# First layer's PLE gate as seven block products, with operands made in the MLP's first pass

## The chip, the cores and the metric

The kernel runs on one core of one Trainium2 chip. The metric is device time in microseconds of one execution. The engines are named as in the profile: PE (TensorE, matmuls; PEld its weight loads), DVE (VectorE), ACT (ScalarE), POOL (GpSimd), SP (SyncE, which here only issues DMAs).

## The reference

Two layers on 1024 tokens with 1024 features. Each layer mixes tokens (layer 0: a gated MLP and a gated delta rule; layer 1: differential attention), then an MLP with squared ReLU, then the PLE step, which the change concerns in layer 0:

```
hn = rms_norm(h, ln_mlp[layer])
h = h + square(relu(hn @ w_mlp1[layer])) @ w_mlp2[layer]
gate = sigmoid(rms_norm(h, ln_ple[layer]) @ w_ple_gate[layer])   # 1024 x 1024
h = h + (p[layer] @ w_ple_proj[layer]) * gate                    # p: 1024 x 256
```

## The kernel before

Activations stand with features on partitions: `acc[m][h]` is feature block m (8 of 128) and token half h (2 of 512). Float32 accuracy comes from splitting every operand into a high part (an ACT cast) and a low part (a DVE subtraction), `split`, L265; `mm3`, L249, then makes three matmuls, high x high, high x low and low x high, each 128x128 by 128x512. The scale of rms_norm is a factor per token and is applied behind the product (`rb[h]`, a row of 512 factors copied to all partitions; `rms`, L300, with `far` sends it through DRAM by two DMAs).

The kernel is written with a tile framework. A tile takes one of its tag's buffers: the rings `w` (12 buffers of 128x512) and `raw` (8), and the slots `c0` to `c13`, `d0`, `B`, `A0` to `A5`, of one buffer each. A new tile under a tag waits until every reader of the old one is done. The framework makes the semaphores and orders each engine's instructions in advance by a timeline that it works out, earlier program text first where several are ready. Each engine then works in that fixed order.

**The MLP** (L333) is two passes of a seven-product block scheme (Strassen's, in Winograd's form). The first pass makes g in 8 chunks of 512 hidden features. A chunk's work is five products of 24 matmuls (`rest`, L472, chunks 0 to 4, named s3, s2, a22, s1, a12 by their left operands in the code) or seven (`chained`, L509, chunks 5 to 7, which also open the next chunk: s2, s1, s3, open1, a22, open2, a12). `product` (L391) splits the weights, then issues 24 matmuls into two PSUM banks. The last product of a chunk, a12, is accumulated into the banks whose earlier content `plus(g22, ...)` has read into the tile g22. `work` (L445) places g12, g21, g22 in the slots c8 to c13: g22 is in c12 and c13, and leaves them when `combine` (L456) has stored it. The seven operands of the second pass go to DRAM by SP's queue (`save`). Between chunks 1 to 4 a side job, `prepare` (L236), makes split attention weights by way of POOL's DMA queue. The second pass (`product2`, L606) runs seven products of 16 steps with 12 matmuls each and gives `acc`; ahead of it `split_p` (L675) transposes p.

**The PLE** (`ple`, L702) is a plain product: for both halves and each feature block m, 8 contraction tiles x 3 = 24 matmuls into a bank. The weights are loaded and split 256 columns at a time, once for each half. `close` (L706) follows: 6 matmuls of the p projection into an `aux` bank (two buffers), then on DVE, ACT, DVE, DVE: times rb, tanh, (1 + t) times the projection, and the sum into acc; a store of h by SP's queue, and `add_square` for the next norm. `put_h` (L277) makes the split operands of the next stage, `values` (L746), which multiplies them with part of the attention weights.

Of the kernel before, what the change touches and what calls it, by code (L numbers as in the profile page):

```python
# [11 lines left out]
F32 = mybir.dt.float32  # L12
# [6 lines left out]
P = 128  # L19
# [26 lines left out]
def f32(ap):  # L46
    return ap.bitcast(F32)
# [92 lines left out]
class Trunk:  # L140
# [107 lines left out]

    def mm3(self, ps, a, b, first, last, more=False):  # L249
# [83 lines left out]
    def mlp(self, x, x_tags, gain, w1, w2, gain_next, h_dram, p, last, side=iter(())):  # L333
# [42 lines left out]
        us, g11s, marks = {}, {}, []  # L376
# [172 lines left out]
        for c in range(NCH):  # L549
            (rest if c < 5 else chained)(c)  # L550
# [10 lines left out]

        pT = self.split_p(p)
# [102 lines left out]
        else:  # L665
            product2(2, y, True)
            add(0, 1, y, put)
            product2(4, x, False, rms)
            self.mlp_mark = self.pe.mark
            add(4, 1, x, put)  # L670
        self.hs[1] = self.hs_new[1]
# [30 lines left out]
    def ple(self, pT, acc, wg, wpj, gain_next, h_dram):  # L702
        nc = self.nc
        gates = []

        def close():  # L706
            h, m, ps = gates.pop(0)
# [4 lines left out]
            nc.vector.tensor_tensor(t, ps, rb[h], ALU.mult)  # L712
# [7 lines left out]
        hs, rb, sqs = list(self.hs), list(self.rb), self.sqs[1]  # L720
        self.new_hs()
        for h in range(2):
            for j in range(4):
                w = self.weight(wg[:, j * 256 : (j + 1) * 256], KT, 256)
                for ml in range(2):
                    m = 2 * j + ml
                    ps = self.mm_ps()
                    for k in range(KT):
                        self.mm3(ps, w.at(k, slice(ml * P, (ml + 1) * P)), hs[h][k], k == 0, k == KT - 1)
                    n = KT * h + m  # L730
                    if n == 0:
                        wq = [self.weight_p(wpj, i) for i in range(4)]
                    if n == 2:
                        rb[1] = self.rms(1, sqs, far=True)[1]
                    while len(gates) > (n < 3):
                        close()
                    gates.append((h, m, ps))
            close()
            for m in range(KT):
                self.put_h(m, h, acc[m][h], gain_next[:, m : m + 1])  # L740
            if h == 0:
                self.take_hs(0, rows=False)
        self.hs[1] = self.hs_new[1]
# [1522 lines left out]
def trunk(tc, x, p, ln_mix_e, w_in_e, gmlp_v_gain, gmlp_ws, gmlp_bs, gdn_conv, gdn_a_log, gdn_dt_bias, gdn_out_gain,  # L2266
          w_out_e, ln_mix_o, w_qkv_o, attn_q_gain, attn_k_gain, diff_lambda, attn_sub_gain, w_out_o, ln_mlp, w_mlp1,
          w_mlp2, ln_ple, w_ple_gate, w_ple_proj, masks, out):
    with ExitStack() as ctx:
# [60 lines left out]
        for layer in range(2):  # L2330
# [18 lines left out]
            acc, pT = T.mlp(x, ((ACC[0:2], ACC[2:4]) if layer else (("A1", "A0"), ("A2", "A3"))), gain[3 * layer + 1], w_mlp1[layer], w_mlp2[layer], gain[3 * layer + 2], h_dram, p[layer, 0], layer == 1, T.prepare(w_qkv_o[0]) if layer == 0 else iter(()))  # L2349
# [4 lines left out]
            T.ple(pT, acc, w_ple_gate[0], w_ple_proj[0], gain[3], h_dram)  # L2354
# [45 lines left out]
```

## Time and profile before

| | |
|---|---|
| median of 3 runs | 2490.58 us (2490.25 to 2491.13) |
| the profiled execution | 2489.38 us |
| its span, first to last instruction | 2487.3 us |
| PE, DVE, ACT, POOL busy | 2476.5, 1828.6, 1341.6, 284.2 us |
| HBM read, written | 318.23 MB, 133.18 MB |
| first pass of the first MLP | till about 775 us |
| its second pass | from 777 to about 1089 us |
| first PLE | about 1089 to 1200 us |

Times in views of the trace count from the start of the span. A row of the view of stretches gives the window, then for each engine the busy time and the number of its instructions, then TensorE's granted clock (1.00 is full speed), the mean busy share of the 16 DMA engines, and GB/s. A row of a group gives its count, busy us and mean ns, then the idle time of the engine before them and what ended it. "q" behind an engine's name means its sequencer, which issues DMAs. The time to landing is counted from the issue of a DMA.

### The profile page before, as it was taken

What the parts mean: (1) busy time and instruction counts of PE and PEld (TensorE: products, weight loads), DVE (VectorE), ACT (ScalarE), POOL (GpSimd) and SP (SyncE); (2) the same over time, 40 slices, a digit from 0 to 9 for tenths busy, and PEclk for the clock granted to TensorE, in tenths of its full rate; (3) what the DMA queues carried; (4) which work ended last, traced back from release to release, by engine and by line L of the source; (5) the groups of instructions that cost most, each with busy time, mean ns of one, the idle gap of its engine ahead of it and who ended that gap; (6) DMA issues with size and microseconds to landing.
All of it is one profiled execution on the core that took longest, in us unless ns stands there. A gap on an engine that the chain in (4) does not pass through costs nothing.

```text
span 2487.3 us, 39296 instructions
## 1 busy us (share of the span) xinstructions
PE 2476.5 (100%) x13465; PEld 2109.8 (85%) x13465; DVE 1828.6 (74%) x3546; ACT 1341.6 (54%) x2732; POOL 284.2 (11%) x331
## 2 busy tenths in 40 slices
PE   9999999999999999999999999999999999999999
PEld 8898998888888888888889999988888888888887
DVE  7868665788756877766848777777877656788586
ACT  6635473655555444644527777765655554445452
POOL 0211220003200001410012232310000000000000
PEclk9999999999999999999999999999999999999999
DMA  8464435469847757964452221467467558656651
GB/s 239 128 186 107 142 123 175 159 201 348 291 166 271 242 165 225 316 190 143 156 171 68 92 71 60 131 236 232 140 220 234 181 169 292 203 186 206 199 171 64
DMA packets 326608, 454.03 MB, mean 183 GB/s; under 512 B 48804, under 2 KB 168584, under 8 KB 326408
## 3 DMA queue, kind: packets, MB, share of 16 engines
q1 hardware_dynamic: 317656, 425.82, 53.2%
q0 software_dynamic: 8192, 25.17, 3.0%
q8 instruction: 106, 1.74, 0.3%
q14 instruction: 94, 0.77, 0.1%
q10 hardware_dynamic: 560, 0.53, 0.1%
HBM read 318.23 MB, written 133.18 MB: 181 GB/s over the span
## 4 chain that ended last, share of the span: by engine, by line
PE 98%; DVE 1%; ACT 0%; issue 0%; DMA 0%; POOL 0%; ACTq 0%; DVEq 0%; POOLq 0%
PE mm L82 85%; PE po L82 3%; PE qk L82 3%; PE tr L85 2%; PE aux L82 2%; DVE lg L1286 0%; PE pks L82 0%; PE pkq L82 0%; PE pvn L82 0%; PE pkk L82 0%; PE pgm L82 0%; PE pab L85 0%; PE pst L82 0%; DMA x<-in_x_dram 0%; PE aux L85 0%
## 5 line engine op out<-in xcount | busy, mean ns | idle before, releaser
L82 PE MATMUL mm<-g,w 128*128 128x512 f32 x2592 | 601.2, 394 | 0.0
L266 ACT CAST w<-raw 128x512 fp32r<-128x512 f32 x586 | 357.7, 617 | 427.9 <-PE mm L82 371.5
L82 PEld LDWEIGHTS mm<-g,w 128*128 128x128 f32 x2592 | 486.5, 188 | 113.5
L82 PE MATMUL mm<-hi,w 128*128 128x512 f32 x1728 | 553.9, 395 | 0.0
L270 DVE TENSOR_TENSOR w<-raw,w 128x512 fp32r<-128x512 f32 x586 | 398.3, 687 | 181.8 <-ACT w L266 165.8
L82 PE MATMUL mm<-w,hi 128*128 128x256 f32 (+2 forms) x2112 | 437.7, 301 | 0.6 <-DVE k L1196 0.6
L82 PEld LDWEIGHTS mm<-hi,w 128*128 128x128 f32 x1728 | 324.3, 188 | 73.6 <-ACT u L422 0.4
L82 PEld LDWEIGHTS mm<-w,hi 128*128 128x128 f32 x2112 | 338.4, 188 | 17.3 <-DVE k L1196 1.3
L82 PE MATMUL mm<-lo,w 128*128 128x512 f32 x864 | 340.0, 394 | 0.0
L82 PE MATMUL mm<-w,lo 128*128 128x256 f32 (+2 forms) x1056 | 316.6, 301 | 0.0
L82 PE MATMUL mm<-t,w 128*128 128x512 f32 x1152 | 271.2, 394 | 0.0
L82 PEld LDWEIGHTS mm<-t,w 128*128 128x128 f32 x1152 | 216.4, 188 | 50.1
L82 PEld LDWEIGHTS mm<-w,lo 128*128 128x128 f32 x1056 | 198.8, 188 | 7.9
L82 PEld LDWEIGHTS mm<-lo,w 128*128 128x128 f32 x864 | 162.6, 188 | 35.9
L270 DVE TENSOR_TENSOR g<-graw,g 128x512 fp32r<-128x512 f32 x216 | 147.6, 685 | 6.3 <-DMA gd<-g 4.1
L266 ACT CAST g<-graw 128x512 fp32r<-128x512 f32 x216 | 132.6, 617 | 23.6 <-DVE g L270 11.0
L311 POOL TENSOR_TENSOR r<-ms,mhalf 128x4 f32<-128x4 f32 x12 | 14.7, 1222 | 959.0 <-DVE ms L309 926.8
L1289 ACT ACTIVATE lg<-lg,nm 128x256 f32<-128x256 f32 (+7 forms) x128 | 99.3, 776 | 41.2 <-DVE nm L1286 40.3
L406 ACT ACTIVATE g<-g 128x512 f32<-128x512 f32 x100 | 63.0, 631 | 87.9 <-DVE g L340 87.6
L244 POOL DMA_DIRECT2D raw<-in_w_qkv_o_dram x64 | 46.3, 725 | 412.4 <-DVE w L270 339.7
L1286 DVE CUSTOM_DVE_ANT_0 lg<-qk,al 128x512 f32<-128x512 f32 (+3 forms) x128 | 74.3, 587 | 23.3 <-PE qk L82 21.2
L82 PE MATMUL mm<-ohi,w 128*128 128x512 f32 x256 | 84.0, 400 | 0.4 <-DVE acc L1506 0.3
(382 smaller groups left out, 3738.4 us busy)
## 6 DMA issues: line engine op xcount, KB each, us to landing
raw<-in_w_mlp_dram SPq DMA_DIRECT2D x352, 256.0 KB, 3.5
graw<-gd SPq DMA_DIRECT2D x224, 256.0 KB, 3.0
gd<-g SPq DMA_DIRECT2D x192, 256.0 KB, 4.0
raw<-in_w_ple_gate_dram SPq DMA_DIRECT2D x76, 256.0 KB, 3.6
acc<-h_dram SPq DMA_DIRECT2D x64, 256.0 KB, 5.0
qk_dram<-w POOLq DMA_DIRECT2D x64, 256.0 KB, 5.3
keep<-in_w_mlp_dram SPq DMA_DIRECT2D x64, 256.0 KB, 5.0
w<-qk_dram SPq DMA_DIRECT2D x64, 256.0 KB, 3.9
```

The source lines that it names most:

```text
L82: self._next(self.engine.matmul(*a, **k))
L85: self._next(self.engine.transpose(*a, **k))
L244: self.nc.gpsimd.dma_start(raw[:, :, j * P : (j + 1) * P], w_qkv[2 * i * P : 2 * (i + 1) * P, c : c + P].rearrange("(k p) m -> p k m", p=P))
L266: inst = self.nc.scalar.copy(hi, src)
L270: inst = (lo_engine or self.nc.vector).tensor_tensor(lo, src, f32(hi), ALU.subtract)
L311: nc.gpsimd.tensor_tensor(r, ms, self.mhalf[:, 0:4], ALU.pow)
L406: nc.scalar.activation(g, src, AF.Relu)
L1286: nc.vector.tensor_tensor_reduce(out=lg[:, k0:k1], in0=ps[:, : k1 - k0], in1=al[:, u0 + k0 : u0 + k1], scale=-0.5 ** (hd + 1), scalar=3.0e ...
L1289: nc.scalar.activation(lg[:, :n], lg[:, :n], AF.Exp, bias=nm[:, r, nch - 1 : nch], scale=-1.0, accum_out=me.sums[:, b, r : r + 1])
```

## The change

The PLE's gate product of layer 0, 1024x1024 by 1024x1024, is cut into 2x2 blocks of 512 and made by the seven-product scheme. Each of the seven is 4 blocks x 4 contraction tiles x 3 matmuls.

*Weight operands.* A generator, `prepare_gate`, loads the four blocks of the gate weights by POOL's queue, one contraction tile k at a time, into the slots c12 (x), c13 (y) and d0 (z), makes the seven left operands with four DVE combinations, splits each into two tiles of the ring `w`, and stores both parts to DRAM by POOL's queue. It has 7 steps for each k. `product` in the MLP takes one step behind each product from chunk 3 on, 31 products in all.

*Token operands.* t1 is made in the last product of the MLP, in place of four puts; t2, t3 and t4 in the PLE, in buffers of operands that are used up.

*The PLE.* Seven sets of 8 ready tiles are loaded by SP's queue into both rings, in the order 1, 2, 5, 6, 7, 4, 3. The closings follow products 2, 7, 4 and 3; three of these four first add a kept partial sum. rb of the second half is made behind product 5. The stores of h move from SP's queue to POOL's.

The core of the diff:

```diff
+    def prepare_gate(self, wg):
+        self.gate_dram = self.dp.tile([7, 4, 2, P, HT], F32, name="gate_dram")
+        def put(n, k, src):
+            parts = [self.wp.tile([P, 1, HT], F32R, tag="w", name=self.nm("w"), bufs=WB)[:, 0] for _ in range(2)]
+            for j, t in enumerate(self.split(src, *parts)):
+                nc.gpsimd.dma_start(self.gate_dram[n - 1, k, j], f32(t))
+        def get(t, j, l, k):
+            nc.gpsimd.dma_start(t, wg[(4 * j + k) * P : (4 * j + k + 1) * P, l * HT : (l + 1) * HT])
...
+        for k in range(4):
+            x, y, z = (self.slot(t, [P, HT], F32, "wg") for t in ("c12", "c13", "d0"))
+            get(y, 1, 1, k)
+            get(x, 0, 1, k)
+            get(z, 0, 0, k)
+            yield
+            put(4, k, y)
+            tt(y, x, y, ALU.add)
+            yield
+            put(5, k, y)
+            tt(x, z, x)
+            yield
+            put(7, k, x)
+            tt(y, y, z)
+            get(x, 1, 0, k)
+            yield
+            put(1, k, z)
+            yield
+            put(6, k, y)
+            yield
+            put(2, k, x)
+            tt(x, x, y)
+            yield
+            put(3, k, x)
@@ mlp: product, and the loop over chunks
                 marks.append(self.pe.mark)
+            for g in beside:
+                next(g, None)
             return ps
...
         for c in range(NCH):
+            if c == 3:
+                beside.append(gates)
             (rest if c < 5 else chained)(c)
...
+        for _ in gates:
+            pass
         pT = self.split_p(p)
@@ mlp: the end, first layer
             product2(2, y, True)
-            add(0, 1, y, put)
+            add(0, 1, y, square)
+            both = self.slot("B", [P, 2, HT], F32, "t1")
+            t1 = [both[:, 0], both[:, 1], self.slot("d0", [P, HT], F32, "t1"), self.sp.tile([P, HT], F32, tag="rb1", name=self.nm("t1"), bufs=1)]
+            def make_t1(k):
+                nc.scalar.activation(t1[k], acc[k][0], AF.Copy, scale=gain_next[:, k : k + 1])
+                nc.vector.scalar_tensor_tensor(t1[k], acc[k][1], gain_next[:, k : k + 1], t1[k], ALU.mult, ALU.subtract)
+                self.hs_new[1][k] = self.split(t1[k], *self.hs_parts(1, k))
+            for k in range(4):
+                rms[9 + 2 * k] = functools.partial(make_t1, k)
             product2(4, x, False, rms)
@@ ple
-                w = self.weight(wg[:, j * 256 : (j + 1) * 256], KT, 256)
...
-                    for k in range(KT):
-                        self.mm3(ps, w.at(k, slice(ml * P, (ml + 1) * P)), hs[h][k], k == 0, k == KT - 1)
...
+        rings = itertools.cycle((("w", WB), ("raw", RB), ("w", WB), ("raw", RB), ("w", WB)))
...
+                    nc.sync.dma_start(f32(a[k][j]), self.gate_dram[n - 1, k, j])
...
+            if plus is not None:
+                ps = tt(t, ps, plus)
+            tt(t, ps, rb[h], ALU.mult)
...
-            nc.sync.dma_start(h_dram[m, :, h * HT : (h + 1) * HT], acc[m][h])
+            nc.gpsimd.dma_start(h_dram[m, :, h * HT : (h + 1) * HT], acc[m][h])
...
+        a = {n: load(n) for n in (1, 2)}
+        x = [self.mm_ps() for _ in R]
+        for q in R:
+            product(q, a[1], b11, x[q], True)
+        u = [self.slot(f"c{8 + q}", [P, HT], F32, "u") for q in R]
+        for q in R:
+            nc.scalar.copy(u[q], x[q])
+        wq = [self.weight_p(wpj, i) for i in R]
+        a[5] = load(5)
+        t2s = right(0, 0, lambda k: scaled(t1[k], 4 + k, 1, t1[k], ALU.subtract))
+        for q in R:
+            close(0, q, product(q, a[2], b21, bank(), True), u[q])
+        a[6] = load(6)
+        w = [self.slot(f"c{8 + q}", [P, HT], F32, "w") for q in R]
+        for q in R:
+            nc.scalar.copy(w[q], product(q, a[5], t1s, bank(), True))
+        a[7] = load(7)
...
+        t3s = right(0, 4, make_t3)
+        t4s = right(1, 0, lambda k: scaled(t1[k], 4 + k, 0, t1[k], ALU.subtract))
+        rb[1] = self.rms(1, sqs, far=True)[1]
...
+        for q in R:
+            product(q, a[6], t2s, x[q])
+            tt(v[q], x[q], w[q])
+        a[4] = load(4)
+        for m in R:
+            put(m, 0)
+        for q in R:
+            close(1, 4 + q, product(q, a[7], t3s, x[q]), w[q])
+        a[3] = load(3)
+        for q in R:
+            close(0, 4 + q, product(q, a[4], t4s, x[q]))
+        for m in R:
+            put(4 + m, 0)
+        for q in R:
+            y = product(q, a[3], b22, bank(), True)
+            if q == 2:
+                self.take_hs(0, rows=False)
+            close(1, q, y, v[q])
+        for m in (4, 5, 6, 7, 0, 1, 2, 3):
+            put(m, 1)
```

More of the change, by code (lines that the diff above doesn't have):

```diff
@@ L670, in mlp @@
             add(4, 1, x, put)
+            self.t1 = t1
         self.hs[1] = self.hs_new[1]
@@ L699, in weight_p, with ple, load, tt @@
         return hi, lo
-    def ple(self, pT, acc, wg, wpj, gain_next, h_dram):
+    def ple(self, pT, acc, wpj, gain, gain_next, h_dram):
         nc = self.nc
-        gates = []
-        def close():
-            h, m, ps = gates.pop(0)
+        R = range(4)
+        t1 = self.t1
+        rings = itertools.cycle((("w", WB), ("raw", RB), ("w", WB), ("raw", RB), ("w", WB)))
+        hs, rb, sqs = list(self.hs), list(self.rb), self.sqs[1]
+        b11, b21, t1s, b22 = hs[0][0:4], hs[0][4:], hs[1][0:4], hs[1][4:]
+        self.new_hs()
+        def load(n):
+            a = []
+            for k in R:
+                a.append([])
+                for j in range(2):
+                    tag, bufs = next(rings)
+                    a[k].append(self.wp.tile([P, 1, HT], F32R, tag=tag, name=self.nm("w"), bufs=bufs)[:, 0])
+                    nc.sync.dma_start(f32(a[k][j]), self.gate_dram[n - 1, k, j])
+            return a
+        def tt(out, a, b, op=ALU.add):
+            nc.vector.tensor_tensor(out, a, b, op)
+            return out
+        def scaled(out, m, h, b, op):
+            nc.vector.scalar_tensor_tensor(out, acc[m][h], gain[:, m : m + 1], b, ALU.mult, op)
+            return out
+        def right(half, k0, make):
+            return [self.split(make(k), *self.hs_parts(half, k0 + k)) for k in R]
+        def product(q, a, b, ps, new=False):
+            for k in R:
+                self.mm3(ps, [y[:, q * P : (q + 1) * P] for y in a[k]], b[k], new and k == 0, k == 3, not new)
+            return ps
+        def bank():
+            return self.aux([P, HT], "sc", "mm")
+        def close(h, m, ps, plus=None):
             pp = self.aux_ps()
```

39 lines of the change are left out of this document (15 added, 24 removed).

## The prediction

> **What bounds the kernel now.** I read the page first: the span, the busy shares and the chain that ended last.
>
> ```profile
> span 2487.3 us, 39296 instructions
> PE 2476.5 (100%) x13465; PEld 2109.8 (85%) x13465; DVE 1828.6 (74%) x3546; ACT 1341.6 (54%) x2732; POOL 284.2 (11%) x331
> PE 98%; DVE 1%; ACT 0%; issue 0%; DMA 0%; POOL 0%; ACTq 0%; DVEq 0%; POOLq 0%
> ```
>
> 98% of the chain is TensorE. Busy time alone would not prove that it runs at its pace, since ends of matmuls are modelled, so I take the chain in order of time inside the PLE and count matmuls against time.
>
> ```profile
> 1116.33 5.55 PE mm L82 x24
> 1121.89 1.38 PE aux L82 x6
> ```
>
> This pair repeats sixteen times, once for each of 8 feature blocks and 2 token halves: 24 gate matmuls in 5.55 us, then 6 of the p projection in 1.38 us. One 512-column matmul costs 5.55 / 24 = 0.231 us, and nothing stands between the pieces. So here a matmul removed is 0.231 us gained, if nothing else becomes late. Then the stages, in the view of stretches: the two busiest chunks of the MLP's first pass, the part of that pass in which the added work must run, and the PLE.
>
> ```profile
> core 0: us, PE busy (x) PEld busy (x) DVE busy (x) ACT busy (x) POOL busy (x), PEclk, DMA share, GB/s
> 580.00:609.00 29.00, 29.00 (x127) 23.61 (x126) 26.78 (x45) 17.13 (x31) 10.37 (x17) 1.00 0.99 343
> 609.00:637.00 28.00, 28.00 (x124) 22.79 (x122) 23.39 (x39) 14.58 (x27) 6.98 (x12) 1.00 1.04 382
> 643.00:775.00 132.00, 132.00 (x571) 107.08 (x570) 87.53 (x139) 74.76 (x132) 9.11 (x15) 1.00 0.61 205
> 1089.00:1200.00 111.00, 111.00 (x490) 90.41 (x489) 75.26 (x120) 49.52 (x85) 2.06 (x2) 1.00 0.45 143
> ```
>
> In each row TensorE issues a matmul every 0.23 us at a granted clock of 1.00. It holds that pace even where DVE was 92% busy (26.78 of 29 us) and where the DMA moved 382 GB/s. Those two rows are the yardstick for what the pass can carry.
>
> **What is removed.** The gate product was 2 halves x 8 blocks x 8 contraction tiles x 3 (high and low parts) = 384 matmuls. Now it is 7 products x 4 blocks x 4 tiles x 3 = 336. The p projection keeps its 96. 48 matmuls go: 48 x 0.231 = **11.1 us**, all on the path. The PLE then takes about 100 us for its 111. This term is safe, as no PE wait in the PLE today has to be removed for it.
>
> The 32 weight splits of the PLE go too, and its 32 loads become 56. DVE there: before 120 operations in the row; by the code, 64 in the closings, 16 puts, 32 low parts and 4 for the projection. After: 64 + 16 + 12 second additions + 4 sums + 12 scaled operands + 12 low parts + 4 = 124. At 75.26 / 120 = 0.63 us that is 78 of 100 us, below the 92% that cost nothing: 0. Loads: 24 more of 0.262 MB on 143 GB/s x 111 us = 15.9 MB makes 22.2 MB in 100 us, 222 GB/s, far under 382: 0. They have time as well. The two rings hold 20 tiles, two and a half operand sets of 8, so a set's last tiles are asked for when the set two before it is done, one product of 48 matmuls (11.1 us) ahead at the least.
>
> ```profile
> L107 SPq DMA_DIRECT2D raw<-in_w_ple_gate_dram x32: 367/368/519, 1065.2 to 1155.0; - x32
> DMA to landing us min/median/max: 2.7/4.0/10.7
> ```
>
> Loads of that size in the old PLE landed in 4.0 us, at worst 10.7, still inside 11.1. Price 0, at worst some 3 us a set if several are slow at once. The stores of h move from SP's queue, where they would stand behind loads that wait for buffers, to POOL's, which is idle there (2.06 us in the row): 0. The four t1 operands replace four puts in the last product of the MLP: 4 operations more on ACT and 4 on DVE, in a stage where PE waits for neither: 0.
>
> **One wait inside the PLE is newly tight.** The second half's scale, rb, is now asked for after the third product (in order of issue) and used in the fifth.
>
> ```profile
> 1106.86 1.04 POOL L311 TENSOR_TENSOR r<-ms,mhalf 128x4 f32<-128x4 f32 x1 [25.18 <-DVE ms L309]
> ```
>
> ```profile
> 1107.93 0.37 SPq L315 DMA_DIRECT2D rd<-r  x1
> 1117.12 0.34 SPq L317 DMA_DIRECT2D rb<-rd  x1
> ```
>
> ```profile
> L317 SPq DMA_DIRECT2D rb<-rd x4: 326/338/339, 51.0 to 1117.1; - x4
> DMA to landing us min/median/max: 4.9/6.7/11.0
> ```
>
> From POOL's power to the second DMA's issue took 1117.12 - 1106.86 = 10.3 us; with 0.5 us for four tiny matmuls and the copy before it and 4.9 to 6.7 us for the landing, some 16.5 us. The third product ends 11.1 + 16.6 + 11.1 = 38.8 us into the PLE (the second carries four projections of 1.38), so rb is there at 55.3. The fourth takes till 49.9, and the first closing of the fifth wants rb at 49.9 + 2.8 + 1.4 = 54.1. DVE waits about 1 us. Queued behind it on DVE are the fifth product's other closings and puts that nobody awaits yet; PE comes to harm only when it wants the first of two projection banks again, at 49.9 + 2 x 4.15 + 2.8 = 61.0, while the chain multiply, tanh, multiply (about 0.7 each) ends by 57.5. Margin 3.5 us: price 0, up to 1 if the landing takes 11.0.
>
> **What is added to the MLP's first pass.** For each of 4 contraction tiles: 4 loads and 14 stores of 0.262 MB on POOL's queue, 7 splits (ACT cast and DVE subtraction) and 4 DVE combinations. Over the pass 72 DMAs with 18.9 MB, 28 casts, 44 DVE operations. They start with chunk 3, at about 609 us, but x and y live in the slots c12 and c13, which hold that chunk's g22, so the bulk runs from 643 to 775 us. There DVE has 139 operations; 183 x 0.6 us (26.78 / 45) = 110 of 132 us, 83%: below 92%, price 0. DMA: 18.9 MB in 132 us is 143 GB/s on 205, so 348 against 382 carried: price 0 in itself, but transfers will land late rather than early. ACT: 75 + 28 x 0.62 = 92 of 132 us: 0. POOL's queue, shared with the preparation of the attention weights that is there already: 16 x 0.72 + 56 x 0.54 us of issue (rows below) on 9 busy, 51 of 132: 0.
>
> What can cost is the **slots**. Each has one buffer, and g22 of chunk c, then tile k's x and y, then g22 of chunk c + 1 must take turns. The last product of a chunk (a12) accumulates into a bank that is first read into g22; if x and y are not done, PE cannot start it. So I compare the length of one turn with the time there is. What a step costs, in the stage itself:
>
> ```profile
> L266 ACT CAST w<-raw 128x512 fp32r<-128x512 f32 x42 | 25.4, 616 | 22.2 <-PE mm L82 19.6 <-DVE u L340 1.7 <-DVE raw L340 0.6
> ```
>
> ```profile
> L270 DVE TENSOR_TENSOR w<-raw,w 128x512 fp32r<-128x512 f32 x43 | 28.9, 686 | 5.2 <-ACT w L266 5.0
> ```
>
> ```profile
> L244 POOL DMA_DIRECT2D raw<-in_w_qkv_o_dram x16: 715/720/732, 602.0 to 648.6; - x16
> DMA to landing us min/median/max: 2.6/5.0/6.8
> ```
>
> ```profile
> L246 POOL DMA_DIRECT2D qk_dram<-w x20: 540/540/575, 598.3 to 665.6; - x20
> DMA to landing us min/median/max: 2.4/5.3/6.9
> ```
>
> A split is 0.62 + 0.69 = 1.31 us. The turn, by its dependences: load 5.0; split 1.31; y = x + y 0.69; split 1.31; split of x 1.31; two store issues ahead of the next load on POOL 1.08; second load into x 5.0; split 1.31; x - y 0.69; split 1.31: **19.0 us** with the median landing, 14.2 with the shortest (2.6), 22.6 with the longest (6.8). With the addition that writes g22, 19.7, 14.9 and 23.3. The time there is: from the last stores of a chunk plus their landing (3.7) to the first matmul of the next chunk's a12.
>
> ```profile
> 638.49 1.44 SPq L411 DMA_DIRECT2D gd<-g  x2
> 677.16 0.94 SPq L411 DMA_DIRECT2D gd<-g  x2
> 713.67 1.30 SPq L411 DMA_DIRECT2D gd<-g  x2
> 754.48 0.39 SPq L411 DMA_DIRECT2D gd<-g  x1
> ```
>
> ```profile
> L411 SPq DMA_DIRECT2D gd<-g x43: 319/339/1277, 659.5 to 776.6; - x43
> DMA to landing us min/median/max: 2.0/3.7/6.8
> ```
>
> ```profile
> 664.11 0.39 PE L82 MATMUL mm<-hi,w 128*128 128x512 f32 x1
> 697.40 0.40 PE L82 MATMUL mm<-hi,w 128*128 128x512 f32 x1
> 736.33 0.39 PE L82 MATMUL mm<-hi,w 128*128 128x512 f32 x1
> 769.74 0.39 PE L82 MATMUL mm<-hi,w 128*128 128x512 f32 x1
> 775.28 1.91 PE L85 MATMUL mm<-ident,t 128*128 128x128 f32 x16
> 776.95 0.48 PE L82 MATMUL mm<-hi,w 128*128 128x512 f32 x1
> ```
>
> Free at 642.2, 680.9, 717.4 and 758.2; wanted at 664.1, 702.9 and 741.9 (the rows at 697.40 and 736.33 begin with 24 matmuls of another product, 5.55 us) and 769.7. That leaves 21.9, 22.0, 24.5 and, in the last chunk, only 11.5 us. At 19.7 the first three turns fit; the fourth is late by 8.2. The order of issue is made by a scheduler that knows of the wait, and two things are free to run ahead of that a12: the 16 transposes (1.7 us from row to row) and the first steps of the second pass (12 matmuls, 2.8 us each). I count the transposes and one step, 4.5 us; 3.7 us remain. At 14.9 the last is late by 3.4, all covered: 0. At 23.3, uncovered, 1.4 + 1.3 + 0 + 11.8 = 14.5. Below nothing it cannot go, since PE has no wait here to lose. I take **3.7 us**, as 5.0 is the median of the nearest row, and keep 0 to 14.5 for the range.
>
> **Sum.** -11.1 + 3.7 = -7.4 us. The profiled execution took 2489.4 us, 2.1 around its span of 2487.3: span 2479.9, that execution 2482.0. The median of the runs is 2490.6, 1.2 above it, so the forecast for it is 2483.2.
>
> **Rivals.**
> (1) *The slots' turn uncovered, at the long landings.* For it: 348 GB/s over 132 us is near what the pass has carried, and DVE already waits for loads there (total us, times, longest):
>
> ```profile
> DVE raw L340 <- DMA raw<-in_w_mlp_dram: 13.8, 9, 3.9
> ```
>
> If the schedule expects a shorter turn than the chip gives, nothing stands ahead of a12, and the loss at a landing of 6 to 6.8 us is 10 to 14.5 us: 2490 to 2494, no change. Against: TensorE has no gap in the row at 382 GB/s.
> (2) *The same turn at the landings of a full POOL queue: slower.* The second load stands behind six stores of its own tile. Over the whole run the transfers of the prepared attention weights, POOL's stores among them, needed up to 10.6 us:
>
> ```profile
> DMA to landing us min/median/max: 2.4/4.5/10.6
> ```
>
> With both loads at 8.7, between 6.8 and that, the turn is 14.2 + 2 x 6.1 = 26.4, with the addition 27.1, and the chunks are late by 5.2 + 5.1 + 2.6 + 15.6 = 28.5, less 4.5 covered: 24 us lost, 2503. It decides against the change from a turn of about 21.5 us, where the lateness, uncovered, sums to 11.1.
> (3) *POOL's queue held up by DVE.* If a POOL DMA could be prepared only between DVE operations, the two loads and the two store issues ahead of the second would wait up to 0.69 each, the turn grows by 2.8 to 21.8, lateness 0.6 + 0.5 + 11.0 = 12.1 less 4.5: 7.6 lost, 2487.1, no change. Against: in the row of stores, from 598 to 666 us, the issue took 540 ns at the median and 575 at most, with DVE 92% busy in part of it. [...]
> (4) *The change does not do what it says in the PLE:* rb or the loads come late often enough to stop PE, 1 to 3 us at three of seven products, some 6 with the 3.7 of the first pass: 2489, no change. Against: the margins above.
>
> **How the numbers follow.** About 0.2%, 5 us, is what a measurement of this kernel can tell from no change. The forecast, with 0 to 6 us lost, has 0.60; rival 1 has 0.21, rival 2 has 0.10, rival 3 has 0.04, rival 4 has 0.05. Faster by over 5 us is the forecast alone, 0.60; within 5 us are rivals 1, 3 and 4, 0.30; slower is rival 2, 0.10. The lower end is nothing lost, 2490.6 - 11.1 = 2479.5; the upper is the price of rival 1 with half of its bound, 2491.0, leaving out rival 2 and the worse half of rival 1. The forecast's own range is 2479.5 to 2485.5.
>
> **What would show it.** Right: 336 gate matmuls, three products of 48 in which no p projection stands, and a PLE of 100 us without gaps; in the first pass the four a12 products follow their s1 or open2 product with no hole, but the last stands behind transposes or a hole of up to 4 us. The landing of the loads from the gate weights near 5 us. Wrong: holes on PE ahead of several a12, with c12 or c13's tiles as releaser; POOL issues much over 0.6 us; a hole in the fifth product's projections. If the total falls by 11 us the turn was shorter than 19 us or wholly covered; if by none, it was over 21.

## The result, and the profile after

The kernel after takes 2552.97 us (median of 4 runs, 2546.85 to 2554.19), the kernel before on the same chip 2490.41: a ratio of 1.0246, with a 95% interval of 1.0228 to 1.0263. It is 62.6 us slower, where 7.4 us less were forecast and 2491.0 was the upper end. The profiled execution took 2554.19 us.

Page of after: the span, busy time of the engines, and the shares of the chain that ended last.

```profile
span 2551.9 us, 39481 instructions
PE 2490.4 (98%) x13417; PEld 2111.0 (83%) x13417; DVE 1866.8 (73%) x3602; ACT 1359.1 (53%) x2756; POOL 334.5 (13%) x419
```

The 48 matmuls are gone: 13465 became 13417. PE's busy time rose all the same, by 14 us, while the span rose by 65: PE both waits and works more slowly (mean granted clock 0.988, before 1.000). To find where, I took the starts of three matmuls from the trace as marks: the first transposition of p (end of the first pass), the last matmul of the second pass, and the first transposition behind `values`. In after, e2, e5 and e15 the order of issue puts 24 matmuls of the first pass behind the first of these marks, in e4 56; at 0.2315 us each they are counted with the first pass. `values` is counted with the PLE, since the order of issue mixes their matmuls at the border. Us more than before in each part, for all kernels of this study, the parts from the one profiled execution of each, the medians from all runs:

| kernel | first pass | second pass | PLE and values | median, us (ratio, 95% interval) |
|---|---|---|---|---|
| before: length of the part | 775.3 | 313.4 | 214.4 | 2490.4 |
| after | +66.5 | +0.4 | -2.3 | 2553.0 (1.0228 to 1.0263) |
| e1 PLE alone | +4.4 | +0.3 | -6.8 | 2489.6 (0.9990 to 1.0009) |
| e2 first pass's job alone | +65.2 | +1.0 | +0.4 | 2558.1 (1.0252 to 1.0293) |
| e3 tiles of its own for x, y | +21.3 | +1.7 | -2.4 | 2511.2 (1.0065 to 1.0099) |
| e4 casts and sums on POOL | +98.6 | +5.1 | -4.5 | 2590.1 (1.0385 to 1.0416) |
| e5 DMAs of the job only | +22.6 | -0.1 | -3.9 | 2504.3 (1.0036 to 1.0076) |
| e6 job in the second pass | +1.7 | +6.8 | -7.8 | 2491.0 (0.9996 to 1.0015) |
| e7 e6, square sums on POOL | +0.8 | +5.1 | -3.9 | 2493.1 (1.0002 to 1.0022) |
| e8 e3, `prepare` in two products | +5.0 | +39.3 | -7.6 | 2529.0 (1.0141 to 1.0171) |
| e9 e3, `prepare` in four products | +2.1 | +8.2 | -5.9 | 2494.1 (1.0006 to 1.0023) |
| e10 e9, 18 DVE operations fewer | +2.0 | +3.3 | -10.7 | 2488.4 (0.9985 to 1.0003) |
| e11 e9, `prepare` spread | +2.3 | +5.4 | -5.0 | 2491.7 (1.0000 to 1.0018) |
| e12 e11, weight sums on POOL | +1.2 | +8.4 | -3.3 | 2496.2 (1.0016 to 1.0033) |
| e13 whole turns in one piece | +90.0 | +0.7 | -4.3 | 2577.6 (1.0337 to 1.0372) |
| e14 e13, `prepare` spread | +94.2 | +4.4 | -2.9 | 2580.2 (1.0349 to 1.0380) |
| e15 parts not in the ring w | +30.0 | +0.4 | -4.3 | 2517.0 (1.0081 to 1.0140) |
| e16 e13, loads ahead, own tiles | +28.7 | +0.7 | -5.4 | 2513.8 (1.0068 to 1.0127) |

So in after nearly all is lost in the first pass, and of the 11.1 us of the PLE 2.3 are left. A column of one execution is only so exact: e9 and e10 have the same second pass, and there it is 8.2 and 3.3. The view of stretches of after, over the part in which the job runs:

```profile
609.00:637.00 28.00, 19.91 (x76) 15.43 (x74) 15.92 (x27) 10.88 (x19) 9.93 (x18) 0.82 0.80 283
637.00:665.00 28.00, 19.68 (x71) 15.03 (x72) 15.73 (x25) 9.48 (x16) 10.63 (x19) 0.88 0.77 265
```

In 609 to 637 PE issued 76 matmuls; before it was 124. No engine is near full, DVE has 57%, and the DMA moves less than before (283 for 382 GB/s). This is not a stage that lacks an engine: everything waits for something else in turn. The view of waits of after names the links, first for 600 to 626 us, then for 600 to 812 (total us, times, longest):

```profile
ACT w L307 <- DMA wg<-in_w_ple_gate_dram: 11.1, 1, 11.1
PEld mm L82 <- ACT w L307: 8.5, 1, 8.5
```

```profile
PEld mm L82 <- ACT w L307: 39.5, 9, 9.0
...
POOL wg L260 <- DMA gd<-g: 27.3, 4, 18.0
...
ACT w L307 <- DMA gate_dram<-w: 16.9, 12, 2.7
```

L307 is the cast of a split, of the gate's weights as of the pass's own. PE waits at its weight splits, not at a12: of its waits over 0.25 us in the first pass behind 600 us, none ends with a write of g22. The three links stand in these rows: a gate load on POOL waits till g22's store has landed and the slot is free (27.3 us in all); ACT's next instruction is the cast of that tile, and stands 11.1 us; behind it in ACT's fixed order are the casts of the weights that PE wants, and PE stands 8.5. The last row is a second way: a cast waits for a tile of the ring w, which holds a gate operand until its store has landed. Two pieces of the chain in order of time (start, us, what), around 612 and around 634 us, show one of each kind:

```profile
612.17 6.54 DMA gd<-g
...
618.78 0.50 issue
...
619.29 2.90 DMA wg<-in_w_ple_gate_dram
...
622.21 0.63 ACT w L307
```

```profile
634.07 5.39 DMA qk_dram<-w
...
639.54 0.31 DVE w L311
639.85 7.80 DMA raw<-in_w_mlp_dram
```

In the second, a store of prepared attention weights keeps a ring tile for 5.39 us; DVE's split waits for it, the raw tile that this split reads comes free late, and only then the next weights of the MLP are asked for, which land 7.80 us later.

### The profile page after: what moved, and what is told of

Its sections match the earlier page's. It is cut to its first block, busy times and chain, and to the rows that moved or that the text cites. A ratio compares the mean times of both kernels' runs of the same rounds, so it can differ in the third digit from the quotient of the medians.

```text
span 2551.9 us, 39481 instructions
## 1 busy us (share of the span) xinstructions
PE 2490.4 (98%) x13417; PEld 2111.0 (83%) x13417; DVE 1866.8 (73%) x3602; ACT 1359.1 (53%) x2756; POOL 334.5 (13%) x419
## 4 chain that ended last, share of the span: by engine, by line
PE 85%; DMA 5%; issue 5%; DVE 4%; POOL 1%; ACT 1%; DVEq 0%; POOLq 0%; SPq 0%; ACTq 0%
PE mm L82 72%; PE po L82 3%; PE qk L82 2%; PE tr L85 2%; DMA raw<-in_w_mlp_dram 1%; PE aux L82 1%; DVE w L311 1%; DMA raw<-in_w_ple_gate_dram 1%; DMA wg<-in_w_ple_gate_dram 1%; DMA gd<-g 1%; DMA gate_dram<-w 0%; DMA qk_dram<-w 0%; DVE lg L1407 0%; PE aux L85 0%; PE pks L82 0%
## 5 line engine op out<-in xcount | busy, mean ns | idle before, releaser
L307 ACT CAST w<-raw 128x512 fp32r<-128x512 f32 x554 | 339.0, 619 | 411.8 <-PE mm L82 319.0
L82 PE MATMUL mm<-hi,w 128*128 128x512 f32 x1696 | 548.3, 398 | 9.2 <-DVE w L311 5.9
L311 DVE TENSOR_TENSOR w<-raw,w 128x512 fp32r<-128x512 f32 x554 | 376.6, 686 | 188.8 <-ACT w L307 167.4
L82 PE MATMUL mm<-t,w 128*128 128x512 f32 x1152 | 286.1, 407 | 37.4 <-ACT w L307 31.9
L82 PEld LDWEIGHTS mm<-t,w 128*128 128x128 f32 x1152 | 224.5, 196 | 95.2 <-ACT w L307 36.2
L307 ACT CAST g<-graw 128x512 fp32r<-128x512 f32 x216 | 133.0, 619 | 23.9 <-DMA gd<-g 10.3
```

Of the source, the lines that this page charges most:

```text
L82: self._next(self.engine.matmul(*a, **k))
L307: inst = self.nc.scalar.copy(hi, src)
L311: inst = (lo_engine or self.nc.vector).tensor_tensor(lo, src, f32(hi), ALU.subtract)
```

## The experiments

The theories, by the letters that the expectations use. A: gate casts that wait for their loads stand in ACT's fixed order ahead of PE's weights. B: the turn of the slots shared with g22 is too long. C: the DMA traffic. D, for the PLE: DVE is full behind it. P, later: a turn is long because its steps stand seven products apart.

**The two halves of the change.** e1 keeps the new PLE; the job is replaced by 56 stores of ready tiles from POOL's queue, so that the gate weights in DRAM are not the right ones. e2 keeps the job and has the old PLE.

> The new PLE with its seven sets of ready tiles, but the job in the MLP's first pass is replaced by 56 plain stores by POOL's queue of tiles that are there already (the gate weights are neither loaded nor combined nor split, so the gates are made from other operands). Theory A, the order of ACT: in the changed kernel ACT stands at a cast of a gate tile whose load is late, and the weight casts behind it starve PE; with no such cast the first pass is as before and the PLE and the stage behind it give what they gave in the changed kernel, -6.8 and +4.5 us: about 2488. Theory B, the turn of the slots (the prediction's): the same, about 2488. Theory C, traffic: 14.7 of the 18.9 MB are still moved, so most of the 67 us of the first pass stay: over 2530.

> The kernel before with the gate job in the first pass alone; what it stores is not read, and the PLE is the old one. All theories: the first pass is longer by about 67 us, as in the changed kernel, so 2557, and the PLE is as before. If it comes out below 2540, the two halves of the change hurt each other.

2489.6 and 2558.1: the job costs what is lost, all of it. The PLE alone gives 6.8 us in its own part and the 56 stores take 4.4 in the first pass.

**Three ways to take one thing from the job.** e3 also loads p only behind the first pass.

```diff
e3 -            x, y, z = (self.slot(t, [P, HT], F32, "wg") for t in ("c12", "c13", "d0"))
   +            x, y, z = self.tmp(), self.tmp(), self.slot("d0", [P, HT], F32, "wg")
e4 -            for j, t in enumerate(self.split(src, *parts)):
   +            nc.gpsimd.tensor_copy(parts[0], src)
   +            nc.gpsimd.tensor_tensor(parts[1], src, f32(parts[0]), ALU.subtract)
   +            for j, t in enumerate(parts):
e5 -            for j, t in enumerate(self.split(src, *parts)):
   -                nc.gpsimd.dma_start(self.gate_dram[n - 1, k, j], f32(t))
   +            for j in range(2):
   +                nc.gpsimd.dma_start(self.gate_dram[n - 1, k, j], src)
```

e4 makes the four combinations on POOL too. e5 leaves out splits and combinations, and stores the loaded tile twice; the slots are shared as in after.

> The changed kernel with x and y in the four temporary tiles, which no g22 shares, and p loaded behind the first pass so that they are free. Theories A and B: the loads no longer wait for a store of g22 to land, so the holes of the first pass are gone but for a few us: 2482 to 2492. Theory C: the traffic is the same, so is the time, over 2535.

> The changed kernel, x and y in c12 and c13 as there, but the gate job's casts, low parts and combinations are POOL's, not ACT's and DVE's. Theory A: no weight cast stands behind a gate tile any more; the holes on weight casts go, and what is left is g22 held up by POOL's longer turn: 2484 to 2510. Theory B: a POOL operation takes about 1.3 us (1294 ns for such a subtraction elsewhere in the kernel) where ACT and DVE take 0.62 and 0.69, so the turn grows from 19 to over 30 us and the time beyond the changed kernel's, over 2553. Theory C: the time stays, about 2550.

> The changed kernel with its loads into c12, c13 and d0 and its 56 stores, on the same queue and in the same slots, but without casts, low parts and combinations: the stores take the loaded tiles themselves (so the operands are not the products', and the gates are others). Theory A2, the turn of the slots, which the first runs leave: whoever waits for the slot, gate work or g22, stands in a fixed order and stops what is behind it; the turn here is two loads and the landing of the stores between them, some 15 to 20 us, so part of the 67 us stays: 2500 to 2530. Theory C, traffic alone: the traffic is all there, so nearly all of the loss: over 2540. If casts in ACT's order were all of it (theory A, which the run on POOL speaks against): about 2488.

e3 brings 41.7 us back, e5 48.6; e4 loses 37 more. With shared slots and all the traffic, but without casts, combinations and tiles of the ring, 22.6 us are lost in the first pass, so slots and traffic alone don't make the 66.5. About half of the 22.6 is the wait that the prediction had named; the waits of e5 from 600 to 800 us:

```profile
PE mm L82 <- DVE g L380: 11.6, 5, 4.1
```

All five end with a write of g22 (`g<-v,mm`). e4 seemed to refute ACT's order (theory A), but it leaves the ring w in common and makes each turn longer (a POOL subtraction takes 1.44 us in e4, the mean of 26; one of DVE's 0.69 in after); I came back to A below.

e4 came out as theory B expected and e5 as A2 did; e3 lies between what A and B expected (2482 to 2492) and what C did (over 2535). Part of what e3 still loses is its own doing: PE stands 2.95 us at the end of the first pass, for p's load (39.05 of 42 us busy from 755 to 797 us, granted clock 0.99), and the edit acts at the same place in layer 1 too. Much of the rest follows two long landings, while both side jobs run. From its chain:

```profile
629.04 9.58 DMA gd<-g
638.76 5.31 DMA raw<-in_w_mlp_dram
...
675.91 9.28 DMA gd<-g
```

The stretch 609 to 637 of e3 moved 372 GB/s, as much as before at that place (382), and 665 to 693 moved 338. These two landings, of 9.58 and 9.28 us, are each followed by a hole of PE, but no run here keeps all else and shortens them.

**Another place for the work.** e6 puts the job into the second pass (tiles of its own, one step at every second step of products 1, 5, 6, 3 and 7). e8 leaves the job in the first pass, with tiles of its own, and puts all of `prepare` into two products of the second (e8 also has e3's edit on p); e9 and e11 spread it thinner.

```diff
e8  -            if 0 < c < 5:
    -                for _ in itertools.islice(side, 4):
    -                    pass
    -                if n in (2, 4) and kt % 2:
    +                if n in (2, 4):
e9  +                if n in (6, 7, 2, 4) and kt % 2:
e11 +                if kt % 2 and (n in (6, 2, 4) or kt > {1: 6, 7: 10}.get(n, NK)):
```

> The changed kernel with x and y in the temporary tiles, and the gate job's steps behind steps of the second pass (products 1, 5, 6, 3 and 7) instead of the products of the first: no shared slots, 18.9 MB over some 220 us, and no other side job beside it. Theories A2 and C: the first pass is as before, the second loses at most 3 us; with -6.8 us of the PLE and +4.5 behind it: 2486 to 2491. If the gate job costs by its ACT and DVE work wherever it stands: over 2500.

> The changed kernel with x and y in the temporary tiles as in the run that came to 2511, and with the preparation of the attention weights (16.8 MB of POOL's traffic in chunks 1 to 4) moved wholly into the second pass. Theory C for what is left there: its holes stand from 631 to 690 us, where both jobs moved 328 to 372 GB/s and transfers landed in up to 9 us; without the other job they go: 2490 to 2496. If they come from the gate job's own casts and low parts, they stay: 2505 to 2512.

> The gate job in the first pass with two tiles of its own (no slot shared with g22), and the attention weights' preparation taken out of that pass: its 32 steps stand at every second of the 16 steps of products 6, 7, 2 and 4 of the second pass. Theory B with traffic (the loss was the turn of the shared slots, and what own tiles left of it were landings of 9 us while both jobs ran at once): the first pass keeps the time of the kernel before, the second pass too or loses up to 3 us, the PLE with the stage behind it gains the 7 to 8 us that the kernel with the job in the second pass showed: 2482 to 2487. Rival (the job's DVE and ACT work alone is too much wherever it stands): the second pass loses 7 us or more as it did with the gate job, 2490 and above.

> As the kernel with both jobs apart, but the preparation of the attention weights stays out of the start of the second pass's product 7, where 10 us of holes stood: 5 steps go to the later half of product 1, 8 to product 6, 3 to the end of product 7, 16 to products 2 and 4. If the start of product 7 was the place (loads of acc, of g and of w2 come together there, and the preparation's raw tiles come out of the same ring): the second pass takes 301 to 304 us (300.6 before, 308.7 with both jobs apart), the total 4 to 8 us less than that, 2485 to 2489 at the median. Rival (the second pass has no room for 16 more steps anywhere): holes of the same sum elsewhere, 2490 or more.

In e8, e9 and e11 the first pass is whole again but for 2 to 5 us, and of e8's 5.0 PE waits 3.3 for p's load. The stretches of e8:

```profile
609.00:637.00 28.00, 28.00 (x123) 22.67 (x122) 25.86 (x42) 16.19 (x30) 7.03 (x13) 1.00 1.00 348
...
1055.00:1100.00 45.00, 28.09 (x106) 21.31 (x105) 24.21 (x40) 16.87 (x30) 29.65 (x31) 0.81 0.78 232
```

In the first row, without `prepare`, DVE is 92% busy and 348 GB/s move, no less than the forecast summed with it, and PE has no gap: such amounts fit. But the 32 steps of `prepare`, at every step of two products of the second pass, cost 39 us there, where the kernel before has 16 of them; at every second step of four products 8.2. That pass lost more than I expected each time, in e6 6.8 us where at most 3 were expected, in e9 and e11 8.2 and 5.4. No version came out faster than the kernel before: e1, e6 and e10 are equal to it within their intervals, and of these only e6 computes the whole.

**What is kept of the PLE's 11.1 us.** In after, behind the PLE, and in the kernel before at the same place, which the prediction had not looked at:

```profile
1257.00:1272.00 15.00, 14.95 (x65) 11.86 (x65) 14.41 (x26) 9.15 (x15) 1.86 (x2) 1.00 0.63 197
1272.00:1285.00 13.00, 9.51 (x29) 6.38 (x28) 13.00 (x20) 5.75 (x10) 3.14 (x3) 0.74 0.33 111
```

```profile
1185.00:1200.00 15.00, 15.00 (x67) 12.14 (x66) 11.32 (x19) 7.53 (x13) 0.00 (x0) 1.00 0.66 212
1200.00:1215.00 15.00, 15.00 (x67) 12.22 (x66) 15.00 (x25) 9.76 (x18) 0.00 (x0) 1.00 0.36 106
1215.00:1230.00 15.00, 15.00 (x71) 12.35 (x70) 15.00 (x25) 5.14 (x10) 0.00 (x0) 1.00 0.63 191
```

Before, DVE was full for the 30 us behind the PLE, and PE just did not have to wait. With PE 11 us earlier at that border it does. e7 moves the square sums of the PLE to POOL (on e6), e12 eight differences of value weights (on e11). e10 instead leaves work out: e9 without the 14 additions of square sums and without the last product's four second additions.

> The run before with one edit: the running sum of squares in the PLE is POOL's, which takes 14 operations from DVE. Theory D: behind the PLE PE waits since DVE has no idle time from about 1257 to 1285 us of the changed kernel's trace, so less DVE work there gives back 2 to 5 us against the run before: 2483 to 2487. Rival: the stores of h that are now in POOL's queue hold up POOL's power, and with it the copies that scale by r: then more work on POOL makes it no better, or 1 to 3 us worse.

> The kernel with both jobs apart, less DVE work in the PLE alone: the additions of the square sums (14) and the four second additions of the last product are left out, so the output is not the reference's. Theory D (behind the PLE DVE has no idle for some 30 us, and that is what keeps 3 to 4 us of the 11.1): some 12 of the 18 additions fall in that stretch, 12 x 0.65 = 8 us of DVE; the holes of TensorE in the first 30 us behind the PLE go, PLE and the stage behind it take 203 to 204 us, and the total is 3 to 4 us under that of the kernel with both jobs apart. Rival (the fixed order of the engines there, or ACT's copies out of the banks, and not DVE's amount of work): the holes stay, the difference is under 1.5 us.

> As the kernel with the preparation spread, and eight of the differences of value weights that the stage behind the PLE needs first are made by POOL, not DVE: 8 x 0.69 = 5.5 us of DVE's work leave the full stretch. Theory D (DVE's amount of work there): PLE and the stage behind it take 204 to 206 us, 3 to 4 us less than in the kernel with the preparation spread, so that the whole is 2481 to 2485. Rival (POOL's own order, with stores of h that wait for DVE, and its slower operation, give it back, as with the square sums): no difference, or up to 3 us slower.

Stretches behind the PLE, of e6, of e9 and of e10:

```profile
1210.00:1225.00 15.00, 13.63 (x58) 10.26 (x57) 15.00 (x24) 6.39 (x11) 3.15 (x3) 1.00 0.38 123
```

```profile
1210.00:1225.00 15.00, 12.24 (x45) 9.31 (x44) 15.00 (x23) 6.22 (x11) 3.15 (x3) 0.89 0.38 126
```

```profile
1204.00:1219.00 15.00, 15.00 (x71) 12.33 (x70) 15.00 (x26) 6.08 (x12) 0.00 (x0) 1.00 0.52 169
```

With 18 DVE operations fewer the hole is gone, PLE and values take 203.7 us (203 to 204 expected), 10.7 of the 11.1 us: DVE's work there is what took them. The profiled execution of e10 was the fastest of its ten, 2483.8, but the medians of e9 and e10 differ by 5.7 us too. How much is taken goes with the granted clock behind the hole, a second price that the rows show: 1.00 in e6, 0.89 in e9, 0.74 in after, with 7.8, 5.9 and 2.3 us kept. With e1 (6.8, at 1.000 over its whole span) that is 6.8 to 7.8 us kept where the clock stays at 1.00, e10 apart, and 2.3 to 5.9 where the row has 0.74 to 0.89 (in e7, e11 and e12, from 1210 to 1225 us, 0.77, 0.89 and 0.89, with 3.9, 5.0 and 3.3 kept). Moving DVE's work to POOL did not help, a miss of mine twice: e7 is 2.1 us slower than e6 at the median, with intervals that overlap, and e12 4.4 slower than e11. In e7 the clock of that row is down to 0.77, in e6 not; in e12 PE waits 4.1 us for a closing on DVE. Why the move did not give what it should was not tested further.

**What carries the wait to PE.** The turns of the shared slots in after, from the first load of a tile's job to its last split, take 44, 43, 31 and 37 us in the trace, not 19.0. The first begins at 617 us, between g22 of chunks 2 and 3, where the forecast put it behind chunk 3's, from 643 on. The job has one step behind each product, and seven steps stand over seven products, 7 x 5.55 = 38.8 us. e13 puts all steps of a tile behind the first product of chunks 3 to 6; e14 does that with `prepare` in the second pass. e15 leaves after as it is, but gives the parts of the splits four general tiles in place of the ring w. e16 is e13 with four load tiles of its own, loaded behind the first product and used behind the third.

```diff
e13 -                next(g, None)
    +                for _ in range(8):
    +                    next(g, None)
    +            beside.clear()
    -            if c == 3:
    +            if 3 <= c < 7:
                     beside.append(gates)
e15 -            parts = [self.wp.tile([P, 1, HT], F32R, tag="w", name=self.nm("w"), bufs=WB)[:, 0] for _ in range(2)]
    +            parts = [self.tp.tile([P, HT], F32R, tag="t", name=self.nm("t")) for _ in range(2)]
e16 +            x, y, z, u = self.tmp(), self.tmp(), self.slot("d0", [P, HT], F32, "wg"), self.tmp()
```

> The slots stay shared with g22, and the operations and DMAs of the job are those of the change; only their place differs: all steps of one contraction tile stand together behind the first product of chunks 3, 4, 5 and 6, where the change hands out one step behind each of seven products. Theory P (the length of the turn is the seven products over which its steps are spread, 38.8 us): the turns shrink from 31 to 44 us to some 20 to 28, and most of the loss goes: 2490 to 2515, of the order of the kernel with tiles of its own (2511) or below. Rival (waits in the fixed order of the engines and 12 weight tiles of the ring taken at once stretch any turn on shared slots): turns over 30 us, 2530 and above.

> As the kernel with whole turns, and the preparation of the attention weights taken out of the first pass to where it stood in the kernel with the preparation spread. Theory P with traffic (what is left with whole turns are long landings while both jobs run): 2486 to 2495, the first pass within 5 us of the kernel before. Rival (the burst itself, with 14 ring tiles and 8 us of DVE in a piece, costs TensorE a hole at each of four chunks): 4 holes of 2 us or more in the first pass, 2497 and above.

> The change as it is, steps one behind each product, slots shared, but the two parts of each split go into the four general tiles and not into the ring of 12 tiles that the pass's weight splits use. Theory A' (a gate cast that waits for its load stands in ACT's fixed order ahead of weight splits): nothing is gained, 2540 to 2565. Rival (the ring of weight tiles carries the wait to TensorE): 20 us or more are gained, 2530 and below.

> All casts, combinations and stores of a tile in one piece behind the third product of chunks 3 to 6, the parts in the common ring; but the four loads go to tiles of their own, shared with no slot of g22, and are issued behind the chunk's first product, two products ahead. Theory A' (TensorE stands because casts wait for their loads in ACT's order): the four holes of 16 to 25 us go, what is left are short holes of the burst, 2490 to 2520. Rival (the burst of 14 weight tiles and 8 us of DVE, or the ring, is what stops TensorE): four holes of 10 us or more stay, 2540 and above.

In e13 the turns are 19.6, 20.9, 19.6 and 19.4 us, as the forecast summed them, and the kernel is slower than after: theory P falls. e14 is no faster than e13, so with whole turns `prepare` beside them is not the cause. Of e13, the waits of 608 to 636 us, then the chain there:

```profile
PEld mm L82 <- ACT w L308: 25.5, 1, 25.5
...
ACT w L308 <- DMA wg<-in_w_ple_gate_dram: 15.7, 2, 11.1
```

```profile
612.40 4.98 DMA gd<-g
...
617.96 3.04 DMA wg<-in_w_ple_gate_dram
...
621.02 0.63 ACT w L308
...
626.88 4.09 DMA wg<-in_w_ple_gate_dram
```

At the first turn PE stands for the landing of g22's store and then for the whole turn, 25.5 us, at the other three 15.6, 21.0 and 18.1: the casts stand together in ACT's order, ahead of PE's next weights, and each waits for its load. In e16 the burst and the ring stay, but the loads are there early, in tiles of their own: 63.8 us come back, and the four holes shrink to 8.1, 6.9, 6.6 and 1.6. That is theory A, shown for the job in one piece; e16 ends the waits of the casts and the sharing with g22 at once, so it doesn't tell these two apart.

e15 was to settle whether the ring matters in after. I expected the order alone; the rival won: 36 us come back. And now the wait that the prediction had named appears; the waits of e15 from 640 to 660 us, then DVE in order of time (start, us, line, what):

```profile
PEld mm L82 <- DVE g L381: 11.5, 1, 11.5
```

```profile
653.36 0.69 DVE L311 TENSOR_TENSOR t<-wg,t 128x512 fp32r<-128x512 f32 x1 [5.80 <-DMA gate_dram<-t]
654.08 0.69 DVE L263 TENSOR_TENSOR wg<-wg,wg 128x512 f32<-128x512 f32 x1
654.80 0.69 DVE L381 TENSOR_TENSOR g<-v,mm 128x512 f32<-128x512 f32 x1
655.50 0.69 DVE L311 TENSOR_TENSOR t<-wg,t 128x512 fp32r<-128x512 f32 x1
656.23 0.69 DVE L381 TENSOR_TENSOR g<-v,mm 128x512 f32<-128x512 f32 x1
```

The two tiles of g22 (`g<-v,mm`) are written right behind the last readers of y and of x, and PE stands 11.5 us for them.

So the 66.5 us of the first pass have no single carrier. Taking away the shared slot gives back 45 of them (48 without e3's wait for p), the shared ring 36, casts, combinations and the ring together 44, `prepare` and the shared slot together 61 to 64. The sum is over 66.5, so they are links of the same chains, each of which can be cut at more than one link. How much of after's loss passes through each, I can't say.

## Why the prediction was wrong, step by step

- **48 matmuls, -11.1 us, "This term is safe".** The count was right. The time was not safe: in none of these kernels that computes the whole does more than 7.8 us of it arrive. What failed here is "as no PE wait in the PLE today has to be removed for it", and with it "78 of 100 us, below the 92% that cost nothing: 0": both look at the PLE alone, and its DVE share is a mean. The 30 us behind the old PLE had DVE at 15.00 of 15 in both rows, and there the gain was kept. Here a term taken off PE was worth its time only up to the engine that was next in that stretch, DVE.
- **rb, the loads, the stores of h: 0.** Right but for 0.5 us, which PE waits for a load in the first product. In the fifth DVE waits 2.1 us for rb, where about 1 was forecast, and PE doesn't wait. The loads of ready operands landed in 5.5 us (median), at most 11.4.
- **t1 in the last product: 0.** Right: in e1, which has t1 and not the job, the second pass is 0.3 us longer, in after 0.4.
- **DVE, ACT, DMA and POOL of the job: each "price 0".** The amounts were right, and the pass can carry such amounts (e8: DVE 92%, 348 GB/s, no gap); the price was not. This is the main step that failed: I charged a cast with its 0.62 us. In ACT's fixed order it costs the time that it waits, and all that stands behind it: in after casts wait 22.1 us for gate loads and 16.9 for ring tiles between 600 and 812 us, and PE's weight loads wait 39.5 us for casts.
- **The slots: 3.7 us, bounds 0 to 14.5.** The turn of 19.0 us is what the trace shows where nothing comes between (19.4 to 20.9 in e13), and the order of issue did put the transposes between a12's matmuls, as forecast. What failed is the sentence "if x and y are not done, PE cannot start it": I took a12 as the only one to wait, and set the turn against the slack of that one product. In after no wait of PE ends with g22; that wait comes only when others are gone, 11.6 us in e5 and some 11 in e15. In after, the steps stand seven products apart, so that the turn was twice as long as its dependences; and the wait for the slot went to POOL's load, to ACT's cast, and from there to PE's weight splits.
- **Left out altogether: the ring w.** The job draws 56 tiles from the 12 that the pass's own splits use, and each is held till its store has landed (2.3 to 6.8 us from issue, 3.2 at the median). No term of my sum had it; e15 shows 36 us.
- **Rival 2, slower by the slots' turn,** had the sign, with 24 us lost where 66.5 were. Its mechanism, landings of 8.7 us, was not it: the loads landed in 3.9 us at the median, where the forecast had 5.0, and in 7.2 at most. Group of the gate loads in after:

```profile
L260 POOL DMA_DIRECT2D wg<-in_w_ple_gate_dram x16: 544/544/759, 308.5 to 798.0; - x16
...
DMA to landing us min/median/max: 2.9/3.9/7.2
```

- **Rivals 1 and 4** were not borne out: the loss is not an uncovered a12, and PE waits for loads 0.5 us in the PLE.
- **Rival 3, POOL's queue held up by DVE:** not borne out. The 56 stores took 542 ns to issue at the median and 577 at most, where the row of before had 540 and 575.

## What to carry to other kernels

Price a side job by what its instructions wait for, not by how long they run: on an engine with a fixed order, a cast whose load waits for a shared buffer stops all that stands behind it (in after ACT stood up to 11.1 us at one, and PE 8.5 behind it), so give such a job load tiles of its own, filled well ahead, and a ring of its own for what it stores (e16 and e15 each did one of the two; no run here did both). List every buffer that the new work takes from a pool that the critical work uses, with how long each is held, landing of the store included. And before you count matmuls taken away as time, look at the stretch in which the next stage begins, not at the stage's mean: an engine at 100% there can keep the gain (DVE, 15.00 of 15 us there: 7.8 of 11.1 us arrived in e6, and 10.7 in e10, with 18 DVE operations fewer).

## What the runs showed of the hardware

In after a hole cost more than its length. Three stretches in and behind the one at 615 us:

```profile
617.00:623.00 6.00, 0.00 (x0) 0.00 (x0) 0.14 (x1) 0.79 (x2) 1.02 (x2) 0.57 0.46 156
623.50:627.50 4.00, 4.00 (x10) 3.13 (x11) 4.00 (x8) 2.55 (x5) 1.90 (x5) 0.50 0.75 239
629.00:636.00 7.00, 7.00 (x32) 5.70 (x31) 4.99 (x8) 5.12 (x9) 3.77 (x7) 1.00 0.88 300
```

Behind the hole of 8.4 us (from the start of one matmul to the next) PE works at a granted clock of 0.50 with 10 matmuls in 4 us (0.43 us from start to start), then at 1.00 with 32 in 7 us. Over the first pass of after the holes, counted beyond the usual 0.23 us from start to start, come to 51.0 us more than before, and matmuls at the lower clock add 14.6, over a quarter on top. The clock goes down to 0.50 seven times in after before the end of the run, five times for 6.8 us, once for 10.2 and once for 13.7. The length of a hole alone does not tell when: the clock fell 2.5 us after the last matmul ahead of the hole at 615 us had ended; at 1276 us, with shorter waits beside it, a wait of 1.9 us was followed by 0.50 from 1276.7 to 1283.5 us; one of 2.2 us at 637 was not, and in e8 PE stood 3.3 us between 755 and 797 us with the clock at 1.00 throughout. What else decides was not shown. The forecast's price of a hole should have had this added.
